# Every third weight chunk's low part on GpSimd in the two mixing parts, the attention and the delta rule

## The chip, the cores and the metric

The kernel runs on one core of one Trainium2 chip. The metric is the device time of one execution in microseconds, median over the runs. The core's engines are TensorE (PE; its weight loads are shown apart as PEld), VectorE (DVE), ScalarE (ACT), GpSimd (POOL) and SyncE (SP, which here only issues loads). Each engine works through its own list of instructions in order and waits on semaphores.

## What is computed

The reference is a stack of two transformer blocks on one sequence of 256 positions and 1024 features, both two layers deep, all in float32. In outline:

```
for l in range(2):                     # first block
    h = modulate(rms_norm(x)); p = h @ w_in
    ret = retention(p); gla_o = gla(p); fox_o = forgetting_attention(p)
    x = x + gate1 * (sum(sigmoid(h @ w_mg) * ([ret, gla_o, fox_o] @ w_br)) @ w_o)
    x = x + gate2 * ((silu(conv(u)) * g) @ w_down)      # u, g = h2 @ w_up
for i in range(2):                     # second block
    x = layer_norm(a * x + 0.5 * swiglu(x))
    x = layer_norm(a * x + (mixer_ab(x) if i == 0 else mixer_c(x)))
    x = layer_norm(a * x + 0.5 * swiglu(x))
    x = x + sigmoid(x @ ple_wg) * (p @ ple_wp)
```

`mixer_ab` is a sliding-window attention beside a gated linear recurrence, `mixer_c` a gated delta rule. The modulation of the first block comes from `silu(c) @ w_ada`.

## The kernel before

All activations stay on chip, features on partitions. What streams through is the weights: a load brings 512 KB (128 x 1024 float32) into one of six `raw` buffers, and each load holds two **chunks** of 128 x 512 (two k-tiles of 256 columns). Float32 products are made of three products in float32r, each operand split in a high part (rounded to float32r) and a low part (what rounding left): `wh*xh + wh*xl + wl*xh`, the three matmuls of `mm3` (L344, L345, L346). So every chunk needs two passes before TensorE can use it: ACT rounds it (L299, `wh`) and DVE subtracts (L300, `wl = raw - wh`). Both land in one of nine `ww` buffers, which a chunk holds until its last matmul. A chunk feeds 12 matmuls of 256 columns.

`run` writes these passes out: the steps of the program are listed first with the chunks that each one eats (`self.steps`), then `feed` hands them out while `ahead` writes loads up to six ahead and the two passes up to four chunks ahead (`AHEAD`) of the matmuls that use them. Chunks of kind `r` are not split: they are rows of `w_ada`, which DVE multiplies with `cact` and sums in one instruction (L413, `ada`); they stand in the same list and are counted with the others. A scheduling layer then places each engine's instructions by the order of writing and by priorities.

The parts of the program, in order and with their times in the profiled execution: the opening (eight units of the first projection at once, with 16 rows of `w_ada`; to about 75 us), the rest of the first mixing part (to 285), with the gates and branch products from about 160, the convolutional feed-forward part, the second mixing part (about 440 to 745, its gates from 620), its feed-forward part, a swiglu, the attention with the recurrence (`mixer_ab`, about 1085 to 1200), two swiglus with the gated embedding between, the delta rule (`mixer_c`, about 1590 to 1810), and the last swiglu and embedding.

POOL has little to do before the change: powers of -0.5 on 2 to 16 columns (L405, `rsqrt`, for the norms, which PE and DVE wait for), some memsets of the delta rule (L1594, L1713, L1714), and two small DMAs in each mixing part. In the delta rule, `xb` is cleared by POOL (L1713) for each half of the heads; the second clearing waits until the first half's `xb` has been written out to memory.

Of the kernel before, what the change touches and what calls it, by code (L numbers as in the profile page):

```python
# [7 lines left out]
F32 = mybir.dt.float32  # L8
# [14 lines left out]
MULT, ADD, SUB, MAX, MIN = ALU.mult, ALU.add, ALU.subtract, ALU.max, ALU.min  # L23
# [92 lines left out]
def _offsets():  # L116
    widths = [("c", 8)]
    for l in range(2):
        for n, w in (("norm1_g", 8), ("norm2_g", 8), ("b_ada", 48), ("ret_norm_g", 4), ("gla_norm_g", 1),
                     ("q_norm_g", 1), ("k_norm_g", 1), ("b_mg", 24), ("b_conv", 22)):  # L120
            widths.append((f"{n}{l}", w))
        widths += [(f"w_conv{l}", 66), (f"b_fox{l}", 1), (f"ln_g{l}", 24), (f"ln_b{l}", 24), (f"ple_bg{l}", 8)]
    widths += [("bcw", 16), ("b_conv_b", 4), ("b_ba", 4), ("b_bx", 4), ("b_lam", 4), ("sinks", 8), ("ccw", 96),
               ("alog", 8), ("dtb", 8), ("c_ng", 1)]
    off, o = {}, 0
    for n, w in widths:
        off[n] = (o, w)
        o += w
    return off, o
# [61 lines left out]
class Prog:  # L191
# [11 lines left out]
    def __init__(self, ctx, tc, io, dbg=None):  # L203
        self.tc, self.nc, self.io, self.dbg = tc, tc.nc, io, dbg
        nc = self.nc
        self.V, self.A, self.G, self.PE = nc.vector, nc.scalar, nc.gpsimd, nc.tensor
        self.steps = []
        self.side = []
        pool = lambda name, **k: ctx.enter_context(tc.tile_pool(name=name, **k))
        self.cp = pool("cst", bufs=1)  # L210
        self.wp = pool("wts", bufs=self.WB)
        self.xp = pool("res", bufs=1)
        self.np_ = pool("nrm", bufs=2)
        self.tp = pool("tiny", bufs=4)
        self.dp = pool("dram", bufs=1, space=bass.MemoryType.DRAM)
        self.pg = pool("psg", bufs=4, space=PSUM)
        self.pm = pool("psm", bufs=4, space=PSUM)
        self.off, npar = _offsets()
        self.par = self.cp.tile([128, npar], F32, name="par")
        self.ident = self.cp.tile([128, 128], F32, name="ident")  # L220
        self.ones = self.cp.tile([128, 272], F32, name="ones")[:, 0:256]
        self.mhalf = self.cp.tile([128, 16], F32, name="mhalf")
        self.mod = [self.cp.tile([128, 48], F32, name=f"mod{l}") for l in range(2)]
        self.cact = self.np_.tile([128, D], F32, name="cact", tag="sy", bufs=1)
        self.gm = {}
        self.x = self.xp.tile([128, 8, S], F32, name="x")
        for k in (0, 4):
            self.dma(self.x[:, k:k + 4, :], io["xT"].rearrange("p (k t) -> p k t", t=S)[:, k:k + 4, :])
        self.dma(self.cact, io["cb"])
        self.dma(self.par, io["par"])  # L230
        self.dma(self.ident, io["c_id"])
        self.V.memset(self.ones, 1.0)
        self.V.memset(self.mhalf, -0.5)
        self.lam = self.cp.tile([128, 8], F32, name="lam")
        self.A.activation(self.lam[:, 0:1], self.mhalf[:, 0:1], AF.Silu)
# [12 lines left out]
        return [("wT",) + c[1:] for c in chunks] if kind == "T" else chunks  # L248

    def step(self, chunks, fn):  # L250
        self.steps.append((chunks, fn))

    def w(self, name, u=0, kt=8, n=256):

# [9 lines left out]
            self.dma(self.dbg[name].rearrange("(k p) t -> p k t", p=128), t)  # L264

    def run(self):
        flat = [c for cs, _ in self.steps for c in cs]
        loads, of = [], []
        for c in flat:
            if "at" not in c[1]:  # L270
                c[1]["at"] = len(loads)
                loads.append(c[1])
            of.append(c[1]["at"])
        got = {}
        nd = ns = nw = i = 0
        c2 = self.CH * 256

        def ahead(upto):
            nonlocal nd, ns, nw
            while nd < min(len(loads), of[min(upto, len(flat)) - 1] + 1 + self.RAW):  # L280
                ld = loads[nd]
                ld["t"] = self.wp.tile([128, 1024], F32, name="raw", tag="raw", bufs=self.RAW)
                self.dma(ld["t"][:, :ld["n"]], ld["ap"])
                nd += 1
            while ns < min(len(flat), upto + self.AHEAD):
                kind, ld, c0, kk, n = flat[ns]
                if of[ns] >= nd:
                    break
                r = ld["t"][:, c0:c0 + kk * n]
                v = lambda t: t.rearrange("p (k n) -> p k n", n=n)  # L290
                if kind == "r":
                    got[ns] = (v(r), kk)
                else:
                    e = kk * n
                    ww = self.wp.tile([128, 2 * c2 + 32], F32R, name="ww", tag=f"ww{nw % self.WB}", bufs=1)
                    o = 32 * ((nw % self.WB + (kind == "wT")) % 2 == self.ODD)
                    nw += 1
                    wh, wl = ww[:, o:o + e], ww[:, o + c2:o + c2 + e]
                    self.A.copy(out=wh, in_=r)  # L299
                    self.V.tensor_tensor(out=wl, in0=r, in1=wh.bitcast(F32), op=SUB)  # L300
                    got[ns] = (v(wh), v(wl), kk)
                ns += 1

        def feed(n):
            nonlocal i
            for _ in range(n):
                ahead(i + 1)
                i += 1
                yield got.pop(i - 1)

        for cs, fn in self.steps:
            it = feed(len(cs))
            fn(it)
            assert next(it, None) is None
# [1691 lines left out]
    def build(self, out):  # L2006
        rest = lambda l, a, b: [lambda j=j: self.step(*self.ada(l, j)) for j in range(a, b)]
        mark = lambda n: self.step([], lambda ws: self.dump(n, self.x))
        for l in range(2):
            self.mix(l, rest(l, 16, 40))  # L2010
            mark(f"d{l}a")
            self.ffn_first(l, rest(l, 40, 48) + (rest(1, 0, 16) + [lambda: self.step([], lambda ws: self.decay_rates())] if l == 0 else []))
            mark(f"d{l}b")

        def store(mp, n=2):
            ks = slice(n * mp, n * mp + n)
            self.dma(out.rearrange("(k p) t -> p k t", p=128)[:, ks, :], self.x[:, ks, :])

        for l in range(2):
            self.ffn_second(l, 1, 0)  # L2020
            if l == 0:
                self.mixer_ab(l)
            else:
                self.mixer_c(l)
            if l == 0:
                ple = self.ple(l, lambda: self.norm_begin(None), self.norm_add)
            else:
                ple = self.ple(l, None, store)
            self.ffn_second(l, 2, 2)
            ple()  # L2030
            mark(f"e{l}d")
        self.run()
# [24 lines left out]
```

## Time and profile before

| | before |
|---|---|
| median of 3 runs | 2014.16 us (2013.57 to 2021.02) |
| the profiled execution's own time | 2018.87 us |
| its span, first to last instruction | 2017.1 us |
| PE busy / DVE / ACT / POOL | 1966.4 / 1534.9 / 1200.6 / 44.4 us |
| memory read | 398.23 MB |

The span is what the profile's rows add up to; the execution's own time is 1.8 us longer, and both lie within the spread of the runs. A busy PE is the union of modelled matmul times and says little about how close the matmuls follow each other.

### The profile page before, as it was taken

Reading aid. Unit: us, or ns where it says so; the run is one execution under the profiler, and the core shown is the slowest. Engines: PE = TensorE matmul, PEld = TensorE weight load, DVE = VectorE, ACT = ScalarE, POOL = GpSimd, SP = SyncE. Lnnn points to the kernel's source line nnn. Section 1 sums busy time; section 2 is a strip of 40 time slices with the busy share of each in tenths; the row PEclk is TensorE's granted clock in tenths of the full one; section 3 lists DMA queues with packets and bytes.
Section 4 is the critical chain, followed back from the end, with each engine's and each line's share of the span. In section 5 each row is a group of like instructions: output and inputs, shape, how many; then the busy total and the mean of one; then the engine's idle time right before and its main releaser. Section 6 shows DMA issues by size and latency. Waiting matters only on the chain.

```text
span 2017.1 us, 42469 instructions
## 1 busy us (share of the span) xinstructions
PE 1966.4 (97%) x16816; PEld 1941.2 (96%) x16816; DVE 1534.9 (76%) x2978; ACT 1200.6 (60%) x2256; POOL 44.4 (2%) x50
## 2 busy tenths in 40 slices
PE   7999999999999999999999999999999998999998
PEld 7999999999999999999999999999999998999998
DVE  8769999887769799866666897667766777687667
ACT  4765466566755466655555776556655576466556
POOL 0100000000000000000000000000000000000000
PEclk9999999999999999999999999999999999999999
DMA  9736977875547877666666446564766543245653
GB/s 332 284 122 204 322 262 241 282 266 197 178 157 249 278 263 232 223 194 196 195 190 198 132 137 202 188 179 148 226 193 193 180 152 114 86 141 200 191 179 110
DMA packets 123852, 404.28 MB, mean 200 GB/s; under 512 B 17114, under 2 KB 24580, under 8 KB 123396
## 3 DMA queue, kind: packets, MB, share of 16 engines
q1 hardware_dynamic: 112884, 397.10, 60.3%
q10 hardware_dynamic: 10416, 3.41, 0.7%
q8 instruction: 131, 2.15, 0.4%
q0 software_dynamic: 352, 1.06, 0.1%
q14 instruction: 69, 0.57, 0.1%
HBM read 398.23 MB, written 3.28 MB: 199 GB/s over the span
## 4 chain that ended last, share of the span: by engine, by line
PE 75%; DVE 12%; DMA 6%; issue 3%; ACT 2%; POOL 1%; SPq 0%; DVEq 0%; ACTq 0%; POOLq 0%
PE psg L344 21%; PE psg L346 21%; PE psg L345 21%; DVE ww L300 4%; DMA raw<-w_ada 3%; DVE raw L413 2%; DMA raw<-w_up 1%; PE psw L344 1%; PE psw L346 1%; PE psw L345 1%; PE psm L1755 1%; DVE nt L385 1%; PE psm L1850 1%; ACT ww L299 1%; DVE hl L385 1%
## 5 line engine op out<-in xcount | busy, mean ns | idle before, releaser
L299 ACT CAST ww<-raw 128x512 fp32r<-128x512 f32 x1304 | 780.3, 616 | 563.7 <-PE psg L346 392.3
L300 DVE TENSOR_TENSOR ww<-raw,ww 128x512 fp32r<-128x512 f32 x1304 | 868.7, 684 | 314.5 <-ACT ww L299 312.9
L346 PE MATMUL psg<-hh,ww 128*128 128x256 f32 x2328 | 651.4, 280 | 5.7 <-DVE ww L300 5.6
L344 PE MATMUL psg<-hh,ww 128*128 128x256 f32 x2328 | 650.2, 280 | 2.6 <-ACT hh L681 1.5
L345 PE MATMUL psg<-hl,ww 128*128 128x256 f32 x2328 | 649.4, 279 | 0.2 <-DVE hl L399 0.2
L346 PEld LDWEIGHTS psg<-hh,ww 128*128 128x128 f32 x2328 | 439.7, 189 | 8.6 <-DVE ww L300 8.2
L344 PEld LDWEIGHTS psg<-hh,ww 128*128 128x128 f32 x2328 | 438.6, 189 | 4.3 <-ACT hh L681 1.8
L345 PEld LDWEIGHTS psg<-hl,ww 128*128 128x128 f32 x2328 | 440.8, 189 | 1.3 <-DVE hl L399 0.5
L346 PE MATMUL psg<-hidh,ww 128*128 128x256 f32 x1056 | 292.6, 277 | 0.2 <-DVE ww L300 0.2
L344 PE MATMUL psg<-hidh,ww 128*128 128x256 f32 x1056 | 292.5, 277 | 0.0
L345 PE MATMUL psg<-hidl,ww 128*128 128x256 f32 x1056 | 292.5, 277 | 0.0
L345 PEld LDWEIGHTS psg<-hidl,ww 128*128 128x128 f32 x1056 | 199.0, 188 | 0.0
L346 PEld LDWEIGHTS psg<-hidh,ww 128*128 128x128 f32 x1056 | 198.4, 188 | 0.4 <-DVE ww L300 0.4
L344 PEld LDWEIGHTS psg<-hidh,ww 128*128 128x128 f32 x1056 | 198.2, 188 | 0.0
L345 PE MATMUL psg<-bl,ww 128*128 128x256 f32 x704 | 194.5, 276 | 0.3 <-DVE bl L399 0.2
L346 PE MATMUL psg<-bh,ww 128*128 128x256 f32 x704 | 194.3, 276 | 0.0
L344 PE MATMUL psg<-bh,ww 128*128 128x256 f32 x704 | 194.0, 276 | 0.0
L413 DVE CUSTOM_DVE_ANT_0 raw<-raw,cact,par 128x1024 f32<-128x1024 f32 x96 | 122.4, 1278 | 22.3 <-DMA raw<-w_ada 22.0
L345 PEld LDWEIGHTS psg<-bl,ww 128*128 128x128 f32 x704 | 132.2, 188 | 0.7 <-DVE bl L399 0.7
L346 PEld LDWEIGHTS psg<-bh,ww 128*128 128x128 f32 x704 | 132.2, 188 | 0.0
L344 PEld LDWEIGHTS psg<-bh,ww 128*128 128x128 f32 x704 | 132.0, 188 | 0.0
L344 PE MATMUL psg<-ww,hh 128*128 128x256 f32 (+1 forms) x336 | 96.7, 292 | 0.0
(456 smaller groups left out, 2997.5 us busy)
## 6 DMA issues: line engine op xcount, KB each, us to landing
raw<-f_up SPq DMA_DIRECT2D x176, 512.0 KB, 4.6
raw<-w_ada SPq DMA_DIRECT2D x96, 512.0 KB, 5.1
raw<-w_up SPq DMA_DIRECT2D x88, 512.0 KB, 5.2
raw<-f_dn SPq DMA_DIRECT2D x80, 512.0 KB, 3.7
raw<-w_in SPq DMA_DIRECT2D x66, 512.0 KB, 4.2
raw<-w_mg SPq DMA_DIRECT2D x46, 512.0 KB, 5.4
raw<-w_down SPq DMA_DIRECT2D x40, 512.0 KB, 4.3
raw<-c_in SPq DMA_DIRECT2D x32, 512.0 KB, 4.5
```

The source lines that it names most:

```text
L299: self.A.copy(out=wh, in_=r)
L300: self.V.tensor_tensor(out=wl, in0=r, in1=wh.bitcast(F32), op=SUB)
L344: mm(ps, wh, xh, start=first, stop=False, skip_group_check=True)
L345: mm(ps, wh, xl, start=False, stop=False, skip_group_check=True)
L346: i = mm(ps, wl, xh, start=False, stop=last, skip_group_check=True)
L385: i = f(*a, **k)
L413: i = self.V.tensor_tensor_reduce(out=w, in0=w, in1=self.cact, scale=1.0, scalar=self.P(f"b_ada{l}", j), op0=MULT, op1=ADD, accum_out=self ...
L1755: mm = lambda o, l_, r_, s: PE.matmul(o, l_, r_, start=s, stop=True, skip_group_check=True)
L1850: PE.matmul(p[:, i, :], l_(i, h), r_(i, h), start=(i == 0), stop=True, skip_group_check=True)
```

## The change

In the steps of `mix`, `mixer_ab` and `mixer_c` (marked by `self.busy`), the subtraction of a chunk goes to POOL where the chunk's place in the list of all chunks leaves 2 when divided by 3; all others stay on DVE. The count runs over `w_ada` rows too: in the opening, where each round of the list has two such rows and four weight chunks, it takes the first and the last of the four.

```
     def step(self, chunks, fn):
-        self.steps.append((chunks, fn))
+        self.steps.append(([(c, self.busy) for c in chunks], fn))
...
     def run(self):
-        flat = [c for cs, _ in self.steps for c in cs]
+        flat = [c for cs, _ in self.steps for c, _ in cs]
+        busy = [b for cs, _ in self.steps for _, b in cs]
...
                     self.A.copy(out=wh, in_=r)
-                    self.V.tensor_tensor(out=wl, in0=r, in1=wh.bitcast(F32), op=SUB)
+                    eng = self.G if busy[ns] and ns % 3 == 2 else self.V
+                    eng.tensor_tensor(out=wl, in0=r, in1=wh.bitcast(F32), op=SUB)
                     got[ns] = (v(wh), v(wl), kk)
...
         for l in range(2):
+            self.busy = True
             self.mix(l, rest(l, 16, 40))
+            self.busy = False
...
             self.ffn_second(l, 1, 0)
+            self.busy = True
             if l == 0:
                 self.mixer_ab(l)
             else:
                 self.mixer_c(l)
+            self.busy = False
```

In the changed kernel the lines stand lower: L299, L300 are L301, L303; L405 is L408; L413 is L416; L1713 is L1716. POOL's list gets 171 subtractions: 62 in the first mixing part (16 of them in the opening), 66 in the second, 15 in `mixer_ab` and 28 in `mixer_c`.

On DVE, in one round of the opening, before the change (`hl` is the low part of a normed activation, `nt` the norm's product, `raw,mod` a row of `w_ada`):

```order
L682 SCALAR_TENSOR_TENSOR hl<-nt,mod_82,hh 128x256
L300 TENSOR_TENSOR ww<-raw,ww 128x512 x3
L413 ISA raw,mod_82<-raw,cact,par 128x1024
L413 ISA mod_82 128x1
L675 SCALAR_TENSOR_TENSOR gm<-mod_82,par 128x1
L413 ISA raw,mod_82<-raw,cact,par 128x1024
L413 ISA mod_82 128x1
L677 SCALAR_TENSOR_TENSOR nt<-x,gm,bc 128x256
L300 TENSOR_TENSOR ww<-raw,ww 128x512
```

and the same round after it:

```order
L685 SCALAR_TENSOR_TENSOR hl<-nt,mod_82,hh 128x256
L303 TENSOR_TENSOR ww<-raw,ww 128x512 x2
L416 ISA raw,mod_82<-raw,cact,par 128x1024
L416 ISA mod_82 128x1
L678 SCALAR_TENSOR_TENSOR gm<-mod_82,par 128x1
L680 SCALAR_TENSOR_TENSOR nt<-x,gm,bc 128x256
L416 ISA raw,mod_82<-raw,cact,par 128x1024
L416 ISA mod_82 128x1
```

Two of four subtractions have left DVE's round, and `nt` has moved ahead of the second row of `w_ada`.

On POOL, in the first mixing part behind the opening, before (`hr` is a power for the head norms, `l` one for the norm of the next part):

```order
L405 TENSOR_TENSOR hr<-hv,mhalf 128x4 x4
L405 TENSOR_TENSOR hr<-hv,mhalf 128x2 x4
L405 TENSOR_TENSOR hr<-hv,mhalf 128x4 x2
L405 TENSOR_TENSOR l_3748<-va,mhalf 128x2
L405 TENSOR_TENSOR l_6257<-va,mhalf 128x2
```

and the end of the same stretch after it:

```order
L408 TENSOR_TENSOR hr<-hv,mhalf 128x4
L303 TENSOR_TENSOR ww<-raw,ww 128x512 x3
L408 TENSOR_TENSOR hr<-hv,mhalf 128x4
L303 TENSOR_TENSOR ww<-raw,ww 128x512 x21
L408 TENSOR_TENSOR l_3748<-va,mhalf 128x2
L303 TENSOR_TENSOR ww<-raw,ww 128x512 x4
L408 TENSOR_TENSOR l_6257<-va,mhalf 128x2
```

The last two `hr` stand around 3 subtractions and 21 follow them (the same place of the second mixing part has 3 and 35). `l_6257`, the norm of the second mixing part's opening pair, now has 4 in front of it.

On POOL in the delta rule, before (`rk`, `rq`, `cf` are powers):

```order
L405 TENSOR_TENSOR rk<-kss,mhalf 128x16
L1825 TENSOR_TENSOR rq_21664<-qs_21666,mhalf 128x8
L1713 MEMSET xb 64x256
L1714 MEMSET xb 64x16
L1825 TENSOR_TENSOR rq_22338<-qs_22340,mhalf 128x8
L405 TENSOR_TENSOR cf<-cf,mhalf 128x4 x4
```

and after:

```order
L408 TENSOR_TENSOR rk<-kss,mhalf 128x16
L303 TENSOR_TENSOR ww<-raw,ww 128x512 x5
L1716 MEMSET xb 64x256
L1717 MEMSET xb 64x16
L1828 TENSOR_TENSOR rq_21664<-qs_21666,mhalf 128x8
L303 TENSOR_TENSOR ww<-raw,ww 128x512 x5
L1828 TENSOR_TENSOR rq_22338<-qs_22340,mhalf 128x8
L408 TENSOR_TENSOR cf<-cf,mhalf 128x4 x2
```

Five subtractions now stand behind the clearing of `xb` and the power `rq`, and the clearing has moved ahead of `rq`.

## Rows read from the trace of the kernel before

**Rows 1.** The page: span, and busy time (share of it) by engine with instructions.
```profile
span 2017.1 us, 42469 instructions
PE 1966.4 (97%) x16816; PEld 1941.2 (96%) x16816; DVE 1534.9 (76%) x2978; ACT 1200.6 (60%) x2256; POOL 44.4 (2%) x50
```

**Rows 2.** Whom PE waited for, whole span: us in total, times, longest.
```profile
PE psg L346 <- DVE ww L300: 8.3, 13, 1.8
...
PE psm L420 <- POOL l L405: 4.4, 3, 2.7
```

**Rows 3.** The same in 0:285, 440:745 and 1085:1200, in this order.
```profile
PE psg L346 <- DVE ww L300: 0.5, 2, 0.2
...
PE psg L346 <- DVE ww L300: 2.9, 3, 1.4
...
PE psg L346 <- DVE ww L300: 0.9, 1, 0.9
```

**Rows 4.** Windows: stretch, length, busy of engines (instructions), PEclk, DMA share, GB/s.
```profile
30.00:75.00 45.00, 44.98 (x381) 44.39 (x380) 40.25 (x79) 27.93 (x54) 0.00 (x0) 1.00 0.94 341
160.00:285.00 125.00, 122.23 (x1036) 121.16 (x1036) 114.98 (x205) 65.62 (x123) 2.01 (x2) 0.99 0.78 271
620.00:745.00 125.00, 122.07 (x1062) 121.25 (x1062) 104.86 (x184) 67.58 (x134) 0.39 (x1) 1.00 0.81 276
```

**Rows 5.** DVE's timeline in one round of the opening: start, length, instructions.
```profile
34.54 0.48 DVE L682 SCALAR_TENSOR_TENSOR hl<-nt,mod,hh 128x256 fp32r<-128x256 f32 x1
34.94 1.89 DVE L300 TENSOR_TENSOR ww<-raw,ww 128x512 fp32r<-128x512 f32 x3
...
40.40 0.48 DVE L682 SCALAR_TENSOR_TENSOR hl<-nt,mod,hh 128x256 fp32r<-128x256 f32 x1
```

**Rows 6.** DVE's groups in 160:285: busy, mean ns | idle before, releaser.
```profile
L300 DVE TENSOR_TENSOR ww<-raw,ww 128x512 fp32r<-128x512 f32 x83 | 54.4, 685 | 5.3 <-ACT ww L299 5.1
L413 DVE CUSTOM_DVE_ANT_0 raw<-raw,cact,par 128x1024 f32<-128x1024 f32 x24 | 30.4, 1280 | 0.6 <-DMA raw<-w_ada 0.5
...
L1294 DVE TENSOR_TENSOR gate<-gate 128x512 f32<-128x512 f32 x8 | 5.5, 683 | 0.0
```

**Rows 7.** Whom DVE waited for in 620:745.
```profile
DVE raw L413 <- DMA raw<-w_ada: 16.2, 6, 4.2
```

**Rows 8.** ACT's rounding in 160:285, as rows 6.
```profile
L299 ACT CAST ww<-raw 128x512 fp32r<-128x512 f32 x82 | 48.3, 619 | 43.4 <-PE psg L346 25.3 <-DMA raw<-w_br 7.1 <-DMA raw<-w_mg 6.8
```

**Rows 9.** POOL's groups, whole span, as rows 6.
```profile
L405 POOL TENSOR_TENSOR hr<-hv,mhalf 128x2 f32<-128x2 f32 x8 | 5.6, 696 | 96.4 <-DVE hv L919 96.4
...
L405 POOL TENSOR_TENSOR rk<-kss,mhalf 128x16 f32<-128x16 f32 x1 | 2.9, 2899 | 41.9 <-DVE lqd L1368 41.9
L1594 POOL MEMSET xx<- 128x2048 f32 x1 | 1.8, 1813 | 198.9 <-PE psg L346 198.9
```

**Rows 10.** Timelines around two POOL powers of four columns.
```profile
80.81 0.68 DVE L300 TENSOR_TENSOR ww<-raw,ww 128x512 fp32r<-128x512 f32 x1
...
80.98 1.41 POOL L405 TENSOR_TENSOR hr<-hv,mhalf 128x4 f32<-128x4 f32 x1 [0.59 <-DVE hv L919]
...
168.87 0.69 DVE L1141 TENSOR_TENSOR qF<-psg,cmix 128x512 f32<-128x512 f32 x1
...
169.06 1.01 POOL L405 TENSOR_TENSOR hr<-hv,mhalf 128x4 f32<-128x4 f32 x1 [27.75 <-DVE hv L919]
```

**Rows 11.** Timeline around a POOL power of two columns.
```profile
749.88 0.68 DVE L300 TENSOR_TENSOR ww<-raw,ww 128x512 fp32r<-128x512 f32 x1
...
750.03 1.08 POOL L405 TENSOR_TENSOR l<-va,mhalf 128x2 f32<-128x2 f32 x1 [129.65 <-DVE va L521]
...
750.60 1.28 DVE L413 CUSTOM_DVE_ANT_0 raw<-raw,cact,par 128x1024 f32<-128x1024 f32 x1
```

**Rows 12.** POOL's timeline in the delta rule.
```profile
1682.47 2.13 POOL L1825 TENSOR_TENSOR rq<-qs,mhalf 128x8 f32<-128x8 f32 x1 [35.79 <-DVE qs L1824]
1693.04 0.30 POOL L1713 MEMSET xb<- 64x256 f32 x1 [8.44 <-DMA dx<-xb]
```

More of the change, by code (lines that the diff above doesn't have):

```diff
@@ L207, in __init__ @@
         self.steps = []
+        self.busy = False
         self.side = []
@@ L250, in step @@
     def step(self, chunks, fn):
-        self.steps.append((chunks, fn))
+        self.steps.append(([(c, self.busy) for c in chunks], fn))
     def w(self, name, u=0, kt=8, n=256):
@@ L266, in run @@
     def run(self):
-        flat = [c for cs, _ in self.steps for c in cs]
+        flat = [c for cs, _ in self.steps for c, _ in cs]
+        busy = [b for cs, _ in self.steps for _, b in cs]
         loads, of = [], []
@@ L299, in ahead @@
                     self.A.copy(out=wh, in_=r)
-                    self.V.tensor_tensor(out=wl, in0=r, in1=wh.bitcast(F32), op=SUB)
+                    eng = self.G if busy[ns] and ns % 3 == 2 else self.V
+                    eng.tensor_tensor(out=wl, in0=r, in1=wh.bitcast(F32), op=SUB)
                     got[ns] = (v(wh), v(wl), kk)
@@ L2009, in build @@
         for l in range(2):
+            self.busy = True
             self.mix(l, rest(l, 16, 40))
+            self.busy = False
             mark(f"d{l}a")
@@ L2020, in build @@
             self.ffn_second(l, 1, 0)
+            self.busy = True
             if l == 0:
@@ L2024, in build @@
                 self.mixer_c(l)
+            self.busy = False
             if l == 0:
```

## The prediction

> **What bounds the kernel now.** I read the page first, then the windows by part, then the waits of PE, then the DVE and POOL rows of the parts the change touches. PE is busy 1966.4 of 2017.1 us [rows 1], so a change on another engine can only give back what PE waits for. Of PE's waits the change aims at one: the last of three matmuls waiting for the low part, 8.3 us in the whole span [rows 2], of which 0.5, 2.9 and 0.9 us lie in the first mixing part, the second and the attention [rows 3]. That is 4.3 us of 2017, and the nine `ww` buffers explain why it is so little: in 160 to 285 ACT's rounding itself stands still 25.3 us because PE has not yet given a buffer back [rows 8], so the split runs ahead of PE by several chunks (one chunk is 12 matmuls at 45/381 = 0.118 us, 1.42 us [rows 4]).
>
> DVE is the near-bound. It is busy 115.0 of 125 us in the gates of the first mixing part and 40.3 of 45 in the late opening [rows 4]. One opening round takes it 40.40 - 34.54 = 5.86 us [rows 5], while PE's 48 matmuls of a round need 48 x 0.118 = 5.66: there DVE, not PE, sets the pace by a little. In the gates of the second mixing part DVE has 20 us idle, but 16.2 of these are waits for rows of `w_ada` at the head of its list [rows 7].
>
> **What is removed.** Each moved subtraction frees DVE by the distance between two such instructions in a run: three take 1.89 us with 0.685 for the last, so 0.60 us each [rows 5, 6]. For 171 that is 103 us of DVE time, nearly all beside a busy PE.
>
> **What is added: the price on POOL.** No row shows a POOL subtraction of 512 columns. The powers give POOL's fixed part for a two-input operation: 0.696 us at 2 columns and 2.899 at 16 make 0.157 per column and 0.38 fixed [rows 9]. A power per column is no guide to a subtraction (512 columns at 0.157 would be 80 us); the nearest row for traffic per column is the memset, 1813/2048 = 0.89 ns per column for one pass [rows 9], 0.45 us for 512. A subtraction makes two reads and a write. If all of it runs at the pace of one pass, it takes 0.38 + 0.45 = 0.83 us; if the three follow one another, 0.38 + 1.36 = 1.74. I take two passes, 1.29 us, since reads and write need not wait for each other. POOL then works 171 x 1.29 = 220 us in all: it has room.
>
> **The price on DVE.** The trace shows that the two engines exclude each other. The power at 80.98 starts while DVE subtracts from two tiles in on-chip memory and takes 1.41 us; the one at 169.06 starts beside a DVE multiply with one operand in PSUM and takes 1.01 [rows 10]. The extra 0.40 us is what was left of the subtraction (81.49 - 80.98 = 0.51) less a start of 0.1. The other direction shows too: DVE's next two-input instruction comes 0.72 us after the subtraction, not 0.60, while POOL's two-column power is in progress [rows 11]. So POOL's reading holds something that a two-input DVE instruction needs, and holds it longer the more it reads. For 512 columns I take a hold of 1.1 us, the operation without its start and its end, with 0.45 (one pass) and 1.74 as ends. A DVE that has two-input work waiting then loses 1.1 for each 0.60 it gave away.
>
> The Trainium skill, page "SBUF — State Buffer", section "Who interferes with whom", says this more strongly: a VectorE instruction with two inputs in SBUF and a GpSimd instruction that reads SBUF share one port as an exclusive lock, and the later one blocks for the whole of the other. For POOL [rows 10] agrees; for DVE [rows 11] shows a delay of 0.12 us under a tiny operation only. By that rule the hold would be the whole 1.29 us and the sum below +20 instead of +13. The page "GPSIMD Engine Reference", section "Performance versus the Vector engine", gives 4497 ns for 2048 columns; a quarter of it, 1.12 us as an estimate, leaves the sum as it is.
>
> **The sum, in us against the profiled execution's 2018.87** (its span is 1.8 less; the median of the runs is 4.7 less, and the shift is the same).
>
> 1. Opening, 16 moved. Nearly all of DVE's list there has two on-chip inputs (I take 0.95): each moved chunk changes DVE by 0.95 x 1.1 - 0.60 = +0.45, 16 make +7. DVE sets the pace already, so +6 arrive.
> 2. Gates of the first mixing part, 24 moved. The two-input rows are 54.4 + 30.4 + 5.5 = 90.3 of 115.0 us, a share of 0.79 [rows 4, 6]: 0.79 x 1.1 - 0.60 = +0.27, 24 make +6.4, and DVE's idle time falls from 10.0 to 3.6. Idle time does not all lie where it is needed; I take half, +3.
> 3. Gates of the second mixing part, 35 moved: +9.4 on a DVE whose 20.1 us of idle time are mostly waits for loads that it can't shift. A third, +3.
> 4. POOL's list. The powers now stand between subtractions, each of which also waits for its load and for ACT. PE already waits 4.4 us for the norm powers [rows 2]; three opening pairs (second mixing part, attention, delta rule) get a subtraction in front, up to 1.29 each, half taken: +2. In the delta rule the clearing of `xb` waited 8.44 us for a DMA [rows 12], and five subtractions now queue behind it; the lead of up to nine chunks (12.8 us) hides most of that: +2.
> 5. Relief: of the 4.3 us in [rows 3] I give back 3: -3.
> 6. The other moved chunks (rest of the mixing parts, attention, delta rule) meet a DVE that is 76% busy on the whole [rows 1]: 0 each; without that room they would cost 0.27 like those of step 2.
>
> Sum: 6 + 3 + 3 + 4 - 3 = **+13**, so 2032 for a profiled execution and 2014.2 + 13 = **2027** for the median.
>
> **Rivals.**
> - *No price on DVE, and relief* (the other side). If POOL's reads hold DVE by no more than they did in [rows 11], DVE loses 103 us of work. All 4.3 us of step 5 come back, the opening drops to PE's 5.66 per round (-1.6), and evacuations that queue behind subtractions gain some, at most as much again: -6 to -11, 2003 to 2008. It decides if the hold is under 0.60/0.95 = 0.63 us. Against it: [rows 10], where four columns already had to wait.
> - *Paid, but hidden.* DVE does stretch, but the chunks' lead covers steps 1 to 4 as it covers the waits now: within 5 us of before, 2009 to 2019. For it: DVE at 92% in 160 to 285 costs PE only 0.5 us today. Against: the opening round, where DVE has no room.
> - *POOL as the late engine.* The hold is the whole three passes (1.74 us), and subtractions stand behind the clearing and the small DMAs. Then step 1 gives 16 x 1.05 = 17, step 2 24 x 0.77 = 18 less 10 idle = 8, step 3 some 9 of 35 x 0.77 = 27, step 4 its double, 8: +42 with all of it, and +27 with half of the last three (12.5) and step 5's relief of 3, 2041 to 2056.
>
> **How the numbers follow.** The forecast, 2019 to 2034 by itself, has 0.47; hidden 0.20; POOL late 0.25; relief 0.08. The range 2008 to 2046 leaves out most of relief and the far end of POOL late. A measurement of this kernel can tell about 0.5%, 10 us, from no change. Slower by more than that: all of POOL late and two thirds of the forecast, 0.55. Within it: the rest of the forecast and hidden, 0.37. Faster: 0.08.
>
> **What would show it.** POOL's subtractions at 1.2 to 1.4 us when alone, longer beside DVE; DVE's two-input instructions that begin under them stretched or late by about 1 us; opening rounds of 6.5 to 6.8 us instead of 5.86; PE waiting for a low part from POOL in the gates; DVE's busy time down by less than 103 us. I am wrong if DVE's rows keep 0.685 us beside POOL, if a POOL subtraction takes 2 us or more, or if POOL's list stalls behind the clearing for longer than the lead.

## The result, and the profile after

The changed kernel takes 2082.41 us (median of 4 runs, 2068.77 to 2089.11) against 2013.87 (4 runs, 2012.12 to 2021.02): a ratio of 1.0306, 95% interval 1.0271 to 1.0342. That is slower by 62 us (55 to 69), where the prediction had +13 and a range up to +32. The sign was right, the size was not.

The page of the changed kernel, the rows that answer to [rows 1]:

```profile
span 2066.7 us, 42721 instructions
PE 1975.6 (96%) x16816; PEld 1945.8 (94%) x16816; DVE 1542.4 (75%) x2807; ACT 1197.6 (58%) x2256; POOL 288.1 (14%) x221
```

171 subtractions left DVE, and DVE is not less busy but 7.5 us more. The groups behind this, whole span (busy, mean ns | idle before, releaser):

```profile
L303 POOL TENSOR_TENSOR ww<-raw,ww 128x512 fp32r<-128x512 f32 x171 | 244.4, 1431 | 1211.3 <-ACT ww L301 1176.6 <-DVE hl L685 28.8 <-issue 5.8
...
L303 DVE TENSOR_TENSOR ww<-raw,ww 128x512 fp32r<-128x512 f32 (+2 forms) x1133 | 818.8, 737 | 332.2 <-ACT ww L301 331.3
L416 DVE CUSTOM_DVE_ANT_0 raw<-raw,cact,par 128x1024 f32<-128x1024 f32 x96 | 131.8, 1375 | 24.1 <-DMA raw<-w_ada 24.0
```

DVE's own subtractions took 685 ns each in the gates before [rows 6] and take 737 in the mean now; the rows of `w_ada` went from 1280 to 1375. Whom PE waited for, as in [rows 2]:

```profile
PE psg L349 <- DVE ww L303: 14.5, 15, 2.2
PE psm L1153 <- DVE kF L1146: 10.0, 4, 5.4
...
PE psm L974 <- DVE w L966: 7.8, 4, 4.2
PE psm L1817 <- ACT v L1966: 7.7, 2, 6.1
PE psg L347 <- ACT ww L301: 5.7, 5, 1.1
...
PE psm L423 <- POOL l L408: 4.1, 4, 2.7
PE psg L349 <- POOL ww L303: 3.8, 8, 0.8
```

The wait that the change aimed at rose from 8.3 to 14.5 us, and 3.8 for POOL's low parts stand beside it. The waits for `kF` (rotated keys) and `w` (scaled heads) are longer too; in the kernel before they were:

```profile
PE psm L1150 <- DVE kF L1143: 2.4, 4, 1.2
...
PE psm L971 <- DVE w L963: 1.3, 2, 1.0
```

PE waits little for POOL by name; most of the growth is in waits for DVE, and some in waits for ACT (`v` in the delta rule, and the roundings).

The windows that answer to [rows 4]:

```profile
30.00:75.00 45.00, 38.01 (x277) 36.22 (x277) 38.00 (x52) 18.95 (x39) 17.43 (x13) 0.92 0.77 259
160.00:285.00 125.00, 113.75 (x957) 111.77 (x956) 110.92 (x164) 59.50 (x111) 41.03 (x27) 0.99 0.72 242
620.00:745.00 125.00, 114.19 (x950) 112.34 (x949) 96.18 (x138) 57.57 (x111) 46.96 (x35) 0.96 0.68 232
```

In 30:75 PE gets 277 matmuls done in place of 381 and DVE has gone from 40.3 to 38.0 us: the stage is slower and no engine in it is full. DVE's timeline of one opening round, as [rows 5]:

```profile
38.26 0.48 DVE L685 SCALAR_TENSOR_TENSOR hl<-nt,mod,hh 128x256 fp32r<-128x256 f32 x1 [0.58 <-ACT hh L684]
39.30 3.07 DVE L303 TENSOR_TENSOR ww<-raw,ww 128x512 fp32r<-128x512 f32 x2 [0.55 <-ACT ww L301]
42.29 1.27 DVE L416 CUSTOM_DVE_ANT_0 raw<-raw,cact,par 128x1024 f32<-128x1024 f32 x1
...
46.07 0.48 DVE L685 SCALAR_TENSOR_TENSOR hl<-nt,mod,hh 128x256 fp32r<-128x256 f32 x1 [0.58 <-ACT hh L684]
```

A round takes 46.07 - 38.26 = 7.81 us. The round of [rows 5], 5.86 us, is one of the two shortest of the kernel before: its seven distances from `hl` to `hl` are 5.86 to 6.45 us, 6.04 in the mean. DVE's two subtractions take 3.07 us instead of 1.29, and DVE stands idle 0.58 + 0.55 = 1.13 us, twice behind ACT, which it did not in the round of [rows 5]. POOL's timeline there has a subtraction beside DVE and one that began while DVE stood idle:

```profile
40.38 1.45 POOL L303 TENSOR_TENSOR ww<-raw,ww 128x512 fp32r<-128x512 f32 x1 [0.26 <-ACT ww L301]
46.62 1.29 POOL L303 TENSOR_TENSOR ww<-raw,ww 128x512 fp32r<-128x512 f32 x1 [4.80 <-DVE hl L685]
```

PE's granted clock, which has two levels here, full (2.4 GHz) and half (1.2 GHz), also falls more often. Its mean over the span, before and after:

```profile
core 0: 2017.1 us, clock 0.994
core 0: 2066.7 us, clock 0.984
```

That is 24 us at the lower level before and 66 after. Leaving out the end of the program, the record shows 5 such stretches before and 13 after, and each time PE had stood idle shortly before the clock fell. The 42 us more at half the clock cost PE at most 21 us, if it had work all that time; no run separates this from the waits that bring it about. From the pages, of the 49.6 us by which the span grew PE stood idle for 40.4 and was busy for 9.2.

### The profile page after: what moved, and what is told of

Same layout as the page of the kernel before. It is cut to its first block, busy times and chain, and to the rows that moved or that the text cites. A ratio compares the mean times of both kernels' runs of the same rounds, so it can differ in the third digit from the quotient of the medians.

```text
span 2066.7 us, 42721 instructions
## 1 busy us (share of the span) xinstructions
PE 1975.6 (96%) x16816; PEld 1945.8 (94%) x16816; DVE 1542.4 (75%) x2807; ACT 1197.6 (58%) x2256; POOL 288.1 (14%) x221
## 3 DMA queue, kind: packets, MB, share of 16 engines
q8 instruction: 131, 2.15, 0.4%
## 5 line engine op out<-in xcount | busy, mean ns | idle before, releaser
L301 ACT CAST ww<-raw 128x512 fp32r<-128x512 f32 x1304 | 776.9, 617 | 533.4 <-PE psg L349 377.5
L303 DVE TENSOR_TENSOR ww<-raw,ww 128x512 fp32r<-128x512 f32 (+2 forms) x1133 | 818.8, 737 | 332.2 <-ACT ww L301 331.3
L303 POOL TENSOR_TENSOR ww<-raw,ww 128x512 fp32r<-128x512 f32 x171 | 244.4, 1431 | 1211.3 <-ACT ww L301 1176.6
L416 DVE CUSTOM_DVE_ANT_0 raw<-raw,cact,par 128x1024 f32<-128x1024 f32 x96 | 131.8, 1375 | 24.1 <-DMA raw<-w_ada 24.0
```

The lines of the kernel that those rows point to most:

```text
L303: eng.tensor_tensor(out=wl, in0=r, in1=wh.bitcast(F32), op=SUB)
L416: i = self.V.tensor_tensor_reduce(out=w, in0=w, in1=self.cact, scale=1.0, scalar=self.P(f"b_ada{l}", j), op0=MULT, op1=ADD, accum_out=self ...
```

## The experiments

Each runs against the kernel before on the same chip, whose median there was 2017 to 2024 us; differences in us are the ratio less 1 times it, with the 95% interval.

**Where the loss is made.** Five kernels move the same chunks, but only in some parts, by where the flag is set:

```
+        self.busy = True
         self.step([c for k in range(8) for c in ...], fn)     # the opening
+        self.busy = False
```

> Only the 16 chunks of the opening go to POOL; everything behind it is as before. Theory (the opening lost more than its DVE price because ACT's roundings of a round now all stand behind the round's hh, so that row of w_ada, hh, roundings, hl and low parts follow one another): +16 us, opening rounds of 7.6 to 7.9 us as in the changed kernel, DVE idle about 1.1 us in each, and no loss behind the opening. Rival (the prediction's step 1, DVE price alone): +6 us and rounds of 6.5 to 6.8. Rival (the opening was slowed by what comes behind it in the lists): under +3 us.

Measured: 1.0070 (1.0044 to 1.0096), +14 us (9 to 19) for 16 chunks. A round takes 46.39 - 38.61 = 7.78 us, with the same two idle times as in the changed kernel, and nothing is lost behind the opening. The prediction's +6 falls.

> The chunks of the two mixing parts behind the opening go to POOL, the opening, the attention and the delta rule stay on DVE. Theory (the loss is made where subtractions stand on POOL): +9 us by the end of the first mixing part and +18 to +19 in the second, +26 to +28 in all, about half of it at the head norms and the retention's cores, and half in the gates. Rival (the prediction's steps 2 and 3 alone): +6 to +8 us, all in the gates. Rival (a lateness inherited from the opening): under +5 in the first mixing part.

Measured: 1.0169 (1.0143 to 1.0195), +34 us (29 to 39) for 112 chunks: more than the theory's 28. The loss is not inherited from the opening.

> Only the chunks of the attention and of the delta rule go to POOL. Theory: +3 us in the attention and +13 to +14 in the delta rule, +16 in all, PE's waits for the convolutions and POOL's clearing of xb longer. Prediction's step 6 with step 4: 0 to +4 us. If the parts add up, this one, the one with the mixing parts and the one with the opening together give the whole loss, less what differs between executions.

Measured: 1.0059 (1.0037 to 1.0080), +12 us (8 to 16) for 43 chunks: the theory's 16 is the end of the interval, the prediction's 4 lies under it. The three parts add up: 14 + 34 + 12 = 60 of 62 us.

> Only the chunks of the gates and branch products of the two mixing parts go to POOL. Prediction's steps 2 and 3: +6 us. Theory 1: +6 to +10 us, what the traces of the changed kernel show there (3.6 and about 4 us). Rival (the gates pay when they no longer inherit lateness from the branches): +15 us or more.

Measured: 1.0054 (1.0031 to 1.0076), +11 us (6 to 15) for 51 chunks. The prediction's +6 lies at the interval's lower end.

> Only the chunks of the mixing parts ahead of the gates go to POOL (projections of the three branches, beside head norms, retention and attention cores), without the opening. Prediction's step 6: 0. Theory 1: +22 to +28 us, the largest loss per chunk of all parts, with PE's waits for kF and for the scaled heads w as long as in the changed kernel.

Measured: 1.0101 (1.0063 to 1.0139), +20 us (13 to 28) for 50 chunks, a little under the theory's figure. Gates and branches make 31 of the 34 us; the 11 chunks behind the gates were not moved by themselves. PE's waits for `kF` and `w` are back without any chunk of the opening or the gates:

```profile
PE psm L976 <- DVE w L968: 7.6, 4, 4.0
PE psm L1155 <- DVE kF L1148: 6.9, 4, 3.4
```

**What the relief is worth.** The moved low passes are left out on both engines:

```
-   eng = self.G if busy[ns] and ns % 3 == 2 else self.V
-   eng.tensor_tensor(out=wl, in0=r, in1=wh..., op=SUB)
+   if not (busy[ns] and ns % 3 == 2): self.V.tensor_tensor(out=wl, ...)
+   # a moved chunk hands out wh twice
```

> Leaves out the low part of the 171 moved chunks altogether: PE takes the high part in its place, as many matmuls as before; neither DVE nor POOL subtracts there. It shows what taking the work off DVE is worth without its price. Theory (the price is what POOL does to DVE and to its own list): faster than before by 4 to 12 us, no opening round above 5.9 us. Rival (the order that the scheduler chooses once DVE's list is shorter costs the time): slower than before by 10 us or more, with opening rounds over 6.5 us though POOL does nothing there.

Measured: 1.0009 (0.9988 to 1.0030), +2 us (-2 to +6). Neither held: DVE's busy time falls to 1442.9 us, by 92, and nothing comes of it. The opening shows how:

```profile
39.68 0.49 DVE L687 SCALAR_TENSOR_TENSOR hl<-nt,mod,hh 128x256 fp32r<-128x256 f32 x1 [0.58 <-ACT hh L686]
40.71 1.29 DVE L304 TENSOR_TENSOR ww<-raw,ww 128x512 fp32r<-128x512 f32 x2 [0.54 <-ACT ww L301]
41.92 1.28 DVE L418 CUSTOM_DVE_ANT_0 raw<-raw,cact,par 128x1024 f32<-128x1024 f32 x1
...
45.71 0.48 DVE L687 SCALAR_TENSOR_TENSOR hl<-nt,mod,hh 128x256 fp32r<-128x256 f32 x1 [0.58 <-ACT hh L686]
```

With two subtractions fewer the rounds from the second on take 6.02 to 6.03 us, as long as the mean of before (6.04). One of the two had stood between `nt` and `hl` and filled the 0.58 us in which ACT makes `hh`; without it DVE waits there. The saved 1.2 us turned into two waits of 0.58 and 0.54 us, and a row behind a wait no longer begins before the one ahead has ended, as 34.94 against 34.54 + 0.48 in [rows 5]. Nor is there much to give back. The window that answers to the first of [rows 4]:

```profile
30.00:75.00 45.00, 44.90 (x388) 44.69 (x386) 33.01 (x64) 28.05 (x55) 0.10 (x1) 1.00 0.95 349
```

DVE is busy for 33.0 us in place of 40.3, but PE is as good as full in both kernels (44.90 and 44.98 of 45 us, with 388 and 381 matmuls), and the loads take 0.95 and 0.94 of the DMA engines. Which of PE, the loads and the waits for ACT ends a round there was not tried apart.

**The hold without the relief, and without the lateness.** DVE makes all low parts again. POOL does something on the raw chunk when DVE is done with it, in the same 171 places:

```
+   self.V.tensor_tensor(out=wl, in0=r, in1=wh..., op=SUB)
+   if busy[ns] and ns % 3 == 2:
+       self.G.tensor_tensor(out=r, in0=r, in1=wh..., op=SUB)   # second subtraction
+       self.G.tensor_copy(out=r, in_=wh...)                    # or: a copy
+       [self.G.memset(r, float(z)) for z in range(2)]          # or: two fills
```

> All low parts stay on DVE as before the change; POOL makes the subtraction of the 171 chunks a second time, over the raw chunk, when DVE has done its own. Nobody waits for this result but the load that takes the raw buffer over, several chunks later. DVE is not relieved. Theory 1 (the price is the stretch of DVE's two-input instructions, and the relief was worth nothing): as slow as the changed kernel or slower, +45 to +80 us, DVE's busy time up by 100 us or more. Theory 2 (the price is that PE and side chains wait for POOL's late low parts): under +15 us, DVE stretched all the same.

Measured: 1.0454 (1.0404 to 1.0503), +92 us (82 to 102), above even theory 1's end. Theory 2 falls: nobody waits for a low part from POOL here, and the loss is half as large again.

> As the kernel with the second subtraction, but POOL copies the rounded chunk over the raw one (one input in place of two), so that its list, its waits and its number of instructions are alike and only what it reads and how long differs. Theory 1 (what POOL reads holds DVE): DVE's stretch falls with POOL's duration; if the copy holds DVE as a subtraction does, two thirds of the other kernel's loss, +25 to +50 us; if one input holds nothing, under +10 us and DVE rows of 0.68 us beside POOL. Theory 2 (POOL's list in order, powers behind other work): the same loss as with the second subtraction.

Measured: 1.0109 (1.0067 to 1.0151), +22 us (14 to 31): by the middle figure just under the 25 to 50 for a copy that holds DVE as long as a subtraction, well over the 10 for none. A copy holds less, as the rows below show.

> All low parts on DVE as before; behind each of the 171 chunks POOL fills the raw chunk with constants, two fills of 512 columns one behind the other, when DVE has read it. POOL's list is as long and its places are the same as with the second subtraction, and a fill reads nothing. Theory 1 (what POOL reads holds DVE, and the list by itself costs little): DVE rows of 0.68 to 0.69 us beside the fills, and +4 to +14 us. Theory 3 (the powers behind other work in POOL's list are most of the price): +20 us or more without any stretch of DVE.

Measured: 1.0002 (0.9978 to 1.0027), 0 us (-4 to +5), below theory 1's 4 to 14 too. POOL is busy 222.1 us in that trace (288.1 in the changed kernel), with more instructions in the same places, though a pair of fills takes 1.11 us and not the 1.29 or more of a subtraction; it costs nothing that can be measured.

The groups of POOL and of DVE with the second subtraction:

```profile
L304 POOL TENSOR_TENSOR raw<-raw,ww 128x512 f32<-128x512 f32 x171 | 280.8, 1644 | 1234.2 <-DVE ww L302 1099.6 <-issue 24.3 <-ACT ww L301 19.9
...
L302 DVE TENSOR_TENSOR ww<-raw,ww 128x512 fp32r<-128x512 f32 x1304 | 942.6, 742 | 303.2 <-ACT ww L301 301.3
```

The same with the copy:

```profile
L304 POOL COPY raw<-ww 128x512 f32<-128x512 f32 x171 | 164.7, 965 | 1279.5 <-DVE ww L302 1167.5 <-ACT ww L301 30.2 <-issue 18.7
...
L302 DVE TENSOR_TENSOR ww<-raw,ww 128x512 fp32r<-128x512 f32 x1304 | 889.8, 700 | 313.8 <-ACT ww L301 311.7
```

And with the two fills:

```profile
L304 POOL MEMSET raw<- 128x512 f32 x342 | 178.7, 524 | 1250.8 <-DVE ww L302 1136.5 <-ACT ww L301 35.5 <-issue 18.1
...
L302 DVE TENSOR_TENSOR ww<-raw,ww 128x512 fp32r<-128x512 f32 x1304 | 869.0, 684 | 314.2 <-ACT ww L301 312.7
```

The hold is read best from three subtractions of DVE in a run, the second or third of them beside POOL. From DVE's timeline with the second subtraction:

```profile
79.69 2.99 DVE L302 TENSOR_TENSOR ww<-raw,ww 128x512 fp32r<-128x512 f32 x3
```

From that with the copy:

```profile
74.10 2.31 DVE L302 TENSOR_TENSOR ww<-raw,ww 128x512 fp32r<-128x512 f32 x3
```

And from that with the fills:

```profile
41.14 1.89 DVE L302 TENSOR_TENSOR ww<-raw,ww 128x512 fp32r<-128x512 f32 x3
```

Three take 1.89 us undisturbed [rows 5]. So the subtraction holds a two-input row of DVE for 1.10 us, the copy for 0.42, the fills not at all.

**POOL's powers.** The change puts the norm powers behind subtractions. Two kernels take them out of POOL's list, one with the change and one without:

```
 def rsqrt(self, out, in_, n):
-    self.G.tensor_tensor(out=out, in0=in_, in1=self.mhalf[:, 0:n], op=ALU.pow)
+    self.V.reciprocal(out=out, in_=in_)
```

> The changed kernel with the powers taken off POOL: DVE makes a reciprocal of the same few columns in their place (another function, so other values, the same data flow). POOL's list holds no power any more. To be set against the kernel before with the same replacement. Theory 1 (most of the price is DVE's stretch): the difference of the two stays at +45 us or more. Theory 3 (most of the price is head norms standing behind subtractions in POOL's list): the difference falls to +30 us or less; the prediction's step 4 gave this 4 us.

> The kernel before with the powers taken off POOL in the same way (reciprocals of the same few columns on DVE, other values). It is the base for the changed kernel with that replacement. All theories: within 15 us of the kernel before, faster if anything, since a power takes POOL 1.0 us and a reciprocal of few columns is short.

Measured: 1.0140 (1.0105 to 1.0176) and 0.9916 (0.9889 to 0.9942), a distance of 0.0224 or 45 us (36 to 54), at the very edge of theory 1, well over theory 3's 30. Some 17 of the 62 us (6 to 28) need the powers on POOL. And the kernel before gains 17 us (12 to 22) by the replacement, a little more than the 15 expected: with another function in place of the power, the opposite of the change, small work taken from POOL to DVE, is the one that is faster. PE's waits in the changed kernel without them:

```profile
PE psm L1153 <- DVE kF L1146: 7.8, 4, 3.7
...
PE psm L974 <- DVE w L966: 1.9, 2, 1.7
```

The wait for `w`, which needs a power, falls from 7.8 to 1.9; that for `kF`, which needs none, only from 10.0 to 7.8.

> The kernel with only the branch chunks of the mixing parts on POOL, and the powers replaced by reciprocals on DVE (another function, the same data flow). To be set against the kernel before with the same reciprocals, 2005.5 us or 0.992 of the kernel before. The branches cost 20 us with the powers on POOL. Theory 1 (DVE's stretch makes the heads late): 12 us or more of the 20 stay, a ratio of 0.998 or more. Theory 3 (the powers stand behind subtractions): 8 us or less stay, a ratio of 0.996 or less.

Measured: 0.9973 (0.9946 to 0.9999), which is 0.0057 or 11.5 us above the kernel before with reciprocals. With the interval, 4 to 19 us stay of 13 to 28: between the two figures by the middle ones, and neither theory is decided. A longer list of POOL costs nothing by itself (the fills), so what the powers take would be a power behind a subtraction that reads; how much of that is the subtraction's longer row and how much the power's own wait for DVE was not separated.

**The order of ACT's list in the opening.** Before, one rounding of a round stood ahead of `hh`; after the change the scheduler put all four behind it. This kernel moves only the opening's chunks and gives their roundings priority, which restores ACT's order:

```
+   with self.tc.high_priority() if moved else nullcontext():
        self.A.copy(out=wh, in_=r)
```

> Only the 16 chunks of the opening go to POOL, and ACT's list has the order of the kernel before: one rounding of a round stands ahead of hh (roundings of moved chunks have priority in the scheduler). DVE's list still has no subtraction between nt and hl. Prediction's step 1 (DVE price alone, the order being as before): rounds of 6.5 to 6.8 us, +6 us. Theory (the hold falls on a ring, whose work lies one behind the other): rounds of 7.1 to 7.5 us, +9 to +11 us. Rival (the order of ACT doesn't matter): rounds of 7.8 us and +14 us as with the opening alone.

Measured: 1.0065 (1.0041 to 1.0089), +13 us (8 to 18), which the time alone does not tell from +14. The rounds do:

```profile
45.13 0.48 DVE L681 SCALAR_TENSOR_TENSOR nt<-x,gm,bc 128x256 f32<-128x256 f32 x1
46.18 0.48 DVE L686 SCALAR_TENSOR_TENSOR hl<-nt,mod,hh 128x256 fp32r<-128x256 f32 x1 [0.58 <-ACT hh L685]
46.69 0.69 DVE L304 TENSOR_TENSOR ww<-raw,ww 128x512 fp32r<-128x512 f32 x1
47.73 1.37 DVE L304 TENSOR_TENSOR ww<-raw,ww 128x512 fp32r<-128x512 f32 x1 [0.35 <-ACT ww L302]
...
52.70 0.48 DVE L681 SCALAR_TENSOR_TENSOR nt<-x,gm,bc 128x256 f32<-128x256 f32 x1
```

52.70 - 45.13 = 7.57 us; the last six rounds take 7.46 to 7.58, at or a little above the end of the theory's 7.1 to 7.5. The order of ACT is worth about 0.2 of some 1.7 us; the wait of 0.58 for `hh` stays in either order.

**The opposite places.** Every third chunk of the feed-forward parts, none elsewhere:

```
+   self.busy = True
    self.ffn_first(...) / self.ffn_second(...)
+   self.busy = False
```

> The opposite choice of places: every third chunk of the feed-forward parts goes to POOL, those of the mixing parts, the attention and the delta rule stay on DVE. DVE is about 61% busy there and PE waits for hardly any chain of DVE work. Theory 1 (a stretch of DVE costs only where PE waits for a chain that runs through DVE's list): 0 to +8 us, though some 250 instructions of DVE are stretched by 1.1 us each. Rival (every moved chunk has its price, as the mean of the changed kernel, 62 us by 171 chunks, 0.36 us): +80 to +100 us. Rival (relief is worth something where POOL has nothing else in its list): faster than before.

Measured: 1.0134 (1.0093 to 1.0174), +27 us (19 to 35) for 263 chunks. All three figures miss: it is 0.10 us per chunk, a quarter of the 0.36, but not nothing. Its page:

```profile
PE 1969.5 (96%) x16816; PEld 1943.0 (95%) x16816; DVE 1447.6 (71%) x2715; ACT 1200.3 (59%) x2256; POOL 402.5 (20%) x313
```

DVE is 87 us less busy than before, and PE waits for it longer (the wait for low parts from DVE is 17.8 us there): a kernel can free an engine and be slower for it. No version here that takes subtractions off DVE and leaves the powers where they were beats the kernel before: leaving them out altogether gains nothing, so there is no gain that a cheaper price on DVE could uncover.

## Why the prediction was wrong

**The unit prices were right.** A POOL subtraction alone takes 1.29 us, as taken; the hold on a two-input DVE row is 1.10 us, as taken. To hit both to the hundredth is partly luck: they were chosen between 0.83 and 1.74 and between 0.45 and 1.74, and a pass over 512 columns, taken as 0.45 us, is 0.52 as a fill. The Trainium skill, page "SBUF — State Buffer", section "Who interferes with whom", says that a DVE instruction with two SBUF inputs contends with a GpSimd instruction that reads SBUF and not with one that only writes it. For two-input rows the fills and the copy agree (0 and 0.42 us). The same page's section "SBUF: two separate sides" has whichever starts first hold the shared pair for the whole instruction; here the row shows 1.10 of 1.29 us.

**The step that failed is the netting**, hold by share less 0.60, with idle time of DVE as cover. How much longer DVE's list became can be read from its busy time, against a kernel with the same DVE work and no reading POOL:

| kernel | DVE longer by, us | slower by, us |
|---|---|---|
| fills | 1535.0 - 1534.9 = 0 | 0 |
| copy | 1567.6 - 1534.9 = 33 | 22 |
| the change | 1542.4 - 1442.9 = 99.5 | 62 |
| second subtraction | 1650.6 - 1534.9 = 116 | 92 |
| low parts left out | 92 shorter | 2 |

By the middle figures a microsecond of stretch costs 0.6 to 0.8 us; a microsecond taken off gives back nothing that can be measured. The prediction set one against the other as if they were the same coin. In fact its price for DVE was too high (a mean of 99.5/171 = 0.58 us per chunk instead of 0.87, so that the net on DVE is nil), and the time lost is nearly five times its sum. Why stretch and relief differ is shown only for the opening: a stretched row delays what stands behind it in the list, while a missing one leaves a gap in which DVE waits for ACT, beside a PE that was full already. The price of the lower clock behind PE's waits (at most 21 us) is in the measured 0.6 to 0.8; the sum has no term for it.

The price also depends on the place. Row by row, against the length of the same operation in the kernel before, DVE is stretched by some 18 us in the kernel with the opening alone, 23 with the branches, 26 with the attention and the delta rule, 32 with the gates and 79 with the feed-forward parts. With their losses of 14, 20, 12, 11 and 27 us a microsecond of stretch costs some 0.8 us in the opening, 0.9 in the branches, 0.5 in the attention and the delta rule, and 0.3 in the gates and the feed-forward parts.

- **Step 1**, +6: +14, from a round of 5.86 us that was shorter than the mean. DVE's work in a round is 7.81 - 1.13 = 6.68 us, inside the forecast 6.5 to 6.8, but the round is 7.81, since 1.13 us of waiting came with it. 6.03 without the passes plus the stretch of 3.07 - 1.29 = 1.78 makes 7.81: the hold is paid in full, the relief not at all.
- **Steps 2 and 3**, +3 each: +11 together. Right in kind, under the mark by 5.
- **Step 4**, +4: a longer list of POOL alone costs 0 (the fills); some 17 of the 62 us (6 to 28) need the powers in it. The clearing of `xb` was not tried by itself.
- **Step 5**, -3: leaving the passes out gives +2 (-2 to +6), so the relief is nil.
- **Step 6**, 0 for "the other moved chunks": the branches lose 20 and the attention with the delta rule 12, 32 of 62 us and the largest miss. "76% busy on the whole" was taken as room. In the branches a stretch costs nearly its whole length, and PE's waits for `kF` and `w` grow there; that the idle quarter of DVE lies outside such chains, with PE at their end, is what these waits suggest and was not shown for each chain.

One such chain in the changed kernel, at 184 to 189 us. POOL's timeline:

```profile
185.78 1.82 POOL L303 TENSOR_TENSOR ww<-raw,ww 128x512 fp32r<-128x512 f32 x1 [8.48 <-ACT ww L301]
187.56 1.00 POOL L408 TENSOR_TENSOR hr<-hv,mhalf 128x4 f32<-128x4 f32 x1
```

And DVE's:

```profile
185.70 0.16 DVE L922 TENSOR_SCALAR hv<-hs 128x4 f32<-128x4 f32 x1
185.76 0.68 DVE L1145 TENSOR_TENSOR w<-w,cmix 128x512 f32<-128x512 f32 x1
188.59 0.69 DVE L1180 TENSOR_TENSOR vT<-vT,hr 128x512 f32<-128x512 f32 x1 [2.15 <-POOL hr L408]
189.20 0.69 DVE L1146 TENSOR_TENSOR qF<-qF,w 128x512 f32<-128x512 f32 x1
```

`hv` is ready at 185.86, but the power starts at 187.56: a subtraction began 0.08 us earlier and had to let `w` on DVE finish first (1.82 us, not 1.29). DVE's next row needs the power and waits 2.15 us, and the rotation behind it waits along, though it needs no power.

**Of the rivals**, "paid, but hidden" falls, as does "no price on DVE". "POOL as the late engine" came nearest in time (2041 to 2056), for reasons that did not hold: the hold is 1.10, not 1.74, and PE waits for POOL's low parts 3.8 us in all. The 2082 us lie above it too.

## What to carry to other kernels

An engine's idle share is no cover for making its instructions longer, where its list runs in order and short chains pass through it: leave the work out first (one run shows what relief is worth) and do it twice (another shows what the disturbance costs), before moving it. A second engine that reads memory beside DVE's two-input work is not free capacity; one that only writes cost nothing here. Where a moved instruction had filled a wait, its time is not saved but turns into that wait.

## What the runs showed of the hardware

The hold on a two-input row follows what POOL reads: 1.10 us for a subtraction of 1.29, 0.42 for a copy of one input of 0.61 us alone (each 0.19 less than POOL's own time), 0 for two fills of 0.52 each. It catches tiny instructions as well: in the opening's trace with ACT's order restored a DVE row of one column beside POOL took 1.13 us instead of 0.16:

```profile
42.87 1.13 DVE L679 SCALAR_TENSOR_TENSOR gm<-mod,par 128x1 f32<-128x1 f32 x1
```

Fills are not harmless to every row of DVE. In the trace with the fills a one-input `TENSOR_SCALAR` of four columns took 0.81 us beside them, where it takes 0.16 otherwise (185.70 above):

```profile
80.87 0.81 DVE L923 TENSOR_SCALAR hv<-hs 128x4 f32<-128x4 f32 x1
```

The seven rows of DVE that are stretched in that trace are all `TENSOR_SCALAR` of 2 to 8 columns, by 2.3 us together.

PE has two paces at the same granted clock. A window in a feed-forward part, where nothing was changed, in the kernel before:

```profile
1300.00:1320.00 20.00, 20.00 (x172) 20.00 (x171) 12.08 (x20) 11.11 (x19) 0.00 (x0) 1.00 0.60 171
```

The same window in the changed kernel, some 40 us earlier in its program, with matmuls of the same shape:

```profile
1300.00:1320.00 20.00, 20.00 (x179) 20.00 (x178) 12.56 (x21) 11.53 (x19) 0.00 (x0) 1.00 0.62 193
```

172 or 179 matmuls in 20 us, both at a clock of 1.00; of the 16 traces read here, 4 have the slower pace in this window and 12 the faster, and it follows no kernel. By the median distance between their starts (near 0.118 us or 0.113), some 90 of 280 groups of 60 matmuls had it before and some 50 after; 40 groups at 0.3 us each are about 12 us by which the profiled pair (2066.7 - 2017.1 = 49.6 us) understates the loss of 62. It may be why runs of one kernel scatter by about 1%, which is not shown. What sets the pace stayed open.
